# Hybrid encoder block on one core: order of projection units around the recurrence's output transpositions, PSUM banks of the first projection pairs, and the gating loads

## The chip, the cores and the metric

The kernel runs on one core of a Trainium2 chip. The metric is device time of one execution in microseconds, the median over several runs. One execution has been profiled in detail, and every row below comes from it.

## The reference, cut to what matters

One layer of an encoder block for 1024 positions of width 1024, in float32. One large input projection feeds a dilated attention and a bidirectional gated linear attention (GLA); both are merged, and a LayerNorm, a squared-ReLU MLP and a second LayerNorm follow. Around the change this is computed:

```python
proj = x @ w_in
(aq, ak, av, gq, gk, gv, gout, lr_f, lr_b, gate_a, gate_g) = split(proj)
la = log_sigmoid(lr @ w_lr + b_lr) / 16
b = cumsum(la)
q_in, k_in = q * exp(b), k * exp(-b)
o = tri(q_in @ k_in.T) @ v + q_in @ state
o = o * rsqrt(mean(o ** 2) + 1e-6)
y_gla = o * gla_norm_g * silu(gout)
```

GLA has 4 heads with keys of 64 and values of 128 columns, and runs forward and backward over the sequence. The state is carried over chunks.

## The kernel before, in words

**Matmul in three parts.** Every float32 operand is split into a rounded high part and a rest (`halve`, L147; `load_w`, L87: ACT casts, DVE subtracts). `mm3` (L97 to L103) does three matmuls for each 128 rows of the inner dimension: high by high, high by low, low by high. L101 to L103 are therefore the lines of nearly all matmuls.

**Order.** The kernel is written as one program, and a scheduler places each instruction in its engine's queue; it may move an instruction past others of its engine where these are not ready in its own estimate. A block under `issue_after(i)` is queued behind instruction `i` on that engine. In the recurrence, `step` (L506) puts each step's PE work behind the PE work of the step before it, so PE's order there is as written. The engines ACT, DVE, POOL and the DMA queue of SP work their queues in order.

**Recurrence** (L521 to L548). For each of four heads PE does: `turn` twice (transpositions of k, L356), `intra(0)` (scores, L396), `kv` twice (L366), on DVE the chain of `states` (L370), the decays of the next head (`pre1`, L317), `intra(1)`, `out(0)` and `out(1)` (outputs, L407 and L408), `pre2` of the next head, and `outt` twice (transpositions of the normalized outputs, L422). The normalization in `out` is: sums of squares on ACT (L412), a small DVE step (L413), a power on POOL (L414), a product on DVE (L415); then `outt` can start. `outt` writes PSUM tiles of the pool "tr", and ACT copies them out (L424).

**Filling.** Between the steps `fill(n)` (L510) issues units of other projections from a list of 28: 8 of 272 columns, 4 of 512 (queries and keys of heads 2 and 3), 16 of 384 (attention values, `att_v`, L430; sets v0 and v1 of 8). Each has 24 matmuls. `extra` (L493) issues the splits of weights behind the unit with a given count. In every head one unit stands between `intra(0)` and `kv`, one behind `pre1`, one behind `intra(1)`, one between `out` and `outt`; after heads 0 and 2 one more behind `outt`; in head 3 the rest stands ahead of `outt`. The split weights lie in rings of 4 ("whi", "wlo").

**PSUM.** Eight banks: three "mm", two "sc", two "tr", one "av".

**First pairs of the Strassen projections** (`proj`, L571). All other columns of `x @ w_in` are done two blocks at a time by seven products on quarter matrices; sums of x (`xsum`, T1 to T4) and of weights (`side`) are made on DVE. p0 and p1 compute the output gate of GLA. Their products use the three "mm" banks in turn (L569). p0's sides S1, S2 and S3 are issued behind all sums of x (L905).

**Gating** (`silu`, L870). Eight pieces; each loads the gate and the head's outputs, and takes a sigmoid on ACT and two products on DVE, at one step of the pairs behind p1. Its three tiles come from the rings of attention scores. The rest of the kernel is not touched.

Of the kernel before, what the change touches and what calls it, by code (L numbers as in the profile page):

```python
# [7 lines left out]
F32 = mybir.dt.float32  # L8
F32R = mybir.dt.float32r
BF16 = mybir.dt.bfloat16  # L10
I32 = mybir.dt.int32
AF = mybir.ActivationFunctionType
OP = mybir.AluOpType
# [6 lines left out]
KT = D // 128  # L20
# [27 lines left out]
def turns(tiles, n):  # L48

    count = itertools.count()  # L50
    return lambda: tiles[next(count) % n]
# [20 lines left out]
def build(tc, io):  # L72
    nc = tc.nc
    V, G, A, T, SP = nc.vector, nc.gpsimd, nc.scalar, nc.tensor, nc.sync
    P = Pools(tc)
    issued = {}
# [5 lines left out]
    scp = P.open("sc", bufs=2, space=PSUM)  # L82
    trp = P.open("tr", bufs=2, space=PSUM)
# [3 lines left out]
    def load_w(src, shape, raw=None):  # L87
        if raw is None:
            raw = wp.tile(shape, F32, tag="raw", bufs=2, name="raw")
            issued["raw"] = SP.dma_start(raw, src)  # L90
        hi = wp.tile(shape, F32R, tag="whi", bufs=4, name="whi")
        A.copy(hi, raw)
        lo = wp.tile(shape, F32R, tag="wlo", bufs=4, name="wlo")
        V.tensor_tensor(lo, raw, hi.bitcast(F32), op=OP.subtract)  # L94
        return hi, lo
# [9 lines left out]
    def mmtile(w=512):  # L105
        return mmp.tile([128, w], F32, tag="mm", name="mm")

    spill = dr.tile([36, 128, S], F32, name="spill")
    yodr = dr.tile([4, 128, S], F32, name="yodr")
    ygdr = dr.tile([4, 128, S], F32, name="ygdr")  # L110
# [36 lines left out]
    def halve(hi, lo, raw, eng=None):  # L147
        (eng or A.copy)(hi, raw)
        V.tensor_tensor(lo, raw, hi.bitcast(F32), op=OP.subtract)
# [17 lines left out]
    for k in range(KT):  # L167
# [5 lines left out]
        else:  # L173
            if k % 2 == 1:
                n = 2 if k < 7 else 1
# [45 lines left out]
    def piece4(name, dtype=F32, shape=(128, S), parts=128):  # L221
        return kp4.tile([parts, *shape[1:]], dtype, tag="k4", bufs=10, name=name)
# [85 lines left out]
    for i in range(2):  # L308
        sl = slice(i * 512, i * 512 + 512)
# [4 lines left out]
    def gla_head(h):  # L314
# [102 lines left out]

        def outt(half):
            on = st["on", half]
            tp = trp.tile([128, 4, 128], F32, tag="tr", name="tr")  # L420
            for c in range(4):
                issued["pe"] = T.transpose(tp[:, c], on[:, c], ident)  # L422
            o = stg.tile([128, 512], F32, tag="stg", name="yo")
            A.activation(o, tp.rearrange("p c t -> p (c t)"), AF.Copy, scale=cols[:, 32 + h:33 + h])  # L424
            SP.dma_start(yodr[h, :, half * 512:half * 512 + 512], o)
# [2 lines left out]


    def att_v(c):  # L430
        w, raws = [], []

        def fetch_raw(i):
            raws.append(xr_t()[:, 0:768].rearrange("p (k f) -> p k f", k=2))
            with tc.issue_after(issued["raw"].ins):
                SP.dma_start(raws[i], io["wtv"][c, i])

        def split(i):
            w.append(load_w(io["wtv"][c, i], [128, 2, 384], raws[i] if raws else None))

        def unit(t):
            r = c * 8 + t - 2
            if 0 <= r < 12:

                with tc.issue_after(issued["raw"].ins):
                    SP.dma_start(tdr[r], trow[r:r + 1].to_broadcast([128, 512]))
            ps = mmtile(384)
            ts = slice(t * 128, t * 128 + 128)
            mm3(ps, [(xh(k, ts), xl(k, ts), w[k // 2][0][:, k % 2], w[k // 2][1][:, k % 2])
                     for k in range(KT)])  # L450
            o = stg.tile([128, 384], F32, tag="stgv", bufs=2, name="stgv")
            A.copy(o, ps)
            SP.dma_start(vdr[ts, c * 384:c * 384 + 384], o)
        return fetch_raw, split, [lambda t=t: unit(t) for t in range(8)]
# [17 lines left out]
    def xsum(nm, k):  # L472
# [7 lines left out]
        if nm != "T4":  # L480
# [12 lines left out]
    extra = {1: [q_load, k_load], 9: [lambda: split0(0), lambda: split0(1)], 10: [lambda: split0(2)],  # L493
             11: [lambda: split0(3)], 13: [lambda: raw1(0), lambda: raw1(1)],
             14: [lambda: raw1(2), lambda: raw1(3)],
             19: [lambda i=i: split1(i) for i in range(4)]}
    for i, (k, n) in enumerate(((0, 0), (1, 0), (2, 0), (3, 0), (0, 1), (1, 1), (2, 1))):
        extra.setdefault(20 + i // 2, []).append(lambda k=k, n=n: after_raw(xload, k, n))
    count = itertools.count()
# [10 lines left out]
    def fill(n):  # L510
        for _ in range(n):
            step(fills.pop(0))
            for f in extra.pop(next(count), ()):
                f()
# [6 lines left out]
    for h, H in enumerate(heads):  # L521
        more = heads[h + 1:h + 2]
        step(H["turn"], 0)
        step(H["turn"], 1)
        step(H["intra"], 0)
        fill(1)
        step(H["kv"], 0)
        step(H["kv"], 1)
        issued["states"] = H["states"]()
        for N in more:  # L530
            step(N["pre1"])
        fill(1)
        step(H["intra"], 1)
        fill(1)
        step(H["out"], 0)
        step(H["out"], 1)
        for N in more:
            N["pre2"]()
        if not more:
            with tc.issue_after(issued["states"].ins):  # L540
                for k in range(4):
                    xsum("T1", k)
        fill(1 if more else len(fills))
        step(H["outt"], 0)
        step(H["outt"], 1)
        if h in (0, 2):
            fill(1)
    with tc.issue_after(issued["on"].ins):  # L548
        for k in range(3):
            xsum("T3", k)  # L550
    for f in (f for n in sorted(extra) for f in extra[n]):
# [13 lines left out]
          for t, n, d in (("whi", 4, F32R), ("wlo", 4, F32R), ("raw", 2, F32))]  # L565
    p_raw = turns(wt[2] + wt[0][:2], 4)
    p_side = turns([wt[1][0], wt[1][1], wt[0][2], wt[1][2], wt[0][3], wt[1][3],
                    px], 7)
    banks = turns([mmtile() for _ in range(3)], 3)  # L569

    def proj(blocks, r, ahead):  # L571

        st, c, ps = {}, {}, {}

# [111 lines left out]
    NP = len(todo)  # L686
    projs = []
    for i, (bl, r) in enumerate(todo):
        projs.append(proj(bl, r, (lambda i=i: projs[i + 2]["raw"]()) if i + 2 < NP else None))


    p0, p1 = projs[:2]
# [2 lines left out]
    for p, n in ((p0, 0), (p1, 0), (p0, 2), (p1, 2)):  # L695
        prep, do = p["steps"][n]
        prep()
        for f in do:
            f()
    with tc.issue_after(issued["on"].ins):  # L700
        for k in range(4):
            if k == 3:
                xload(k, 1)
                xsum("T3", k)
            xsum("T2", k)
# [163 lines left out]

    def silu(h, hf):  # L870
        sl = slice(hf * 512, hf * 512 + 512)
        g, y, sg = (n().rearrange("p a b -> p (a b)") for n in (e_t, et_t, e_t))
        SP.dma_start(g, spill[4 + h, :, sl])
        SP.dma_start(y, yodr[h, :, sl])
        A.activation(sg, g, AF.Sigmoid)
        with tc.issue_after(issued["add"].ins):
            V.tensor_tensor(y, y, g, op=OP.mult)
            V.tensor_tensor(y, y, sg, op=OP.mult)
        SP.dma_start(ygdr[h, :, sl], y)

    tiles = [att(g, t) for g in (2, 1, 0) for t in range(8)]

# [4 lines left out]
                tiles[n][part]()  # L887


    a, b = p0["steps"][1], p0["steps"][4]  # L890
    steps = [(a[0], b[1]), p0["steps"][3], (b[0], a[1]), *p0["steps"][5:]] + [p1["steps"][n] for n in (1, 3, 4, 5, 6)]
    n0 = len(steps) + 14
    for p in projs[2:]:
        steps += p["steps"]
# [3 lines left out]
        units.setdefault(n0 + 1 + i * (n1 - n0) // 27, []).append(lambda i=i: visit(i))  # L898
    for i in range(8):

        units.setdefault(n0 - 12 + i, []).append(lambda i=i: silu(i // 2, i % 2))
    units[n0].append(tiles[0][0]) if n0 in units else units.setdefault(n0, [tiles[0][0]])
    for i in range(3):
        steps[i][0]()
    fed = []  # L905
    wbt, pa = {}, {}

# [819 lines left out]
```

## Time and profile before

| what | value |
|---|---|
| median of 3 runs | 1412.26 us (1409.19 to 1415.08) |
| the profiled execution | 1410.22 us |
| its span, first to last instruction | 1408.4 us |
| mean granted TensorE clock | 0.994 of full |
| PE busy | 1377.2 us, 98% |
| DVE busy | 1012.7 us, 72% |
| ACT busy | 627.4 us, 45% |

Engines: PE is TensorE's matmuls, PEld its weight loads, DVE VectorE, ACT ScalarE, POOL GpSimd, SP the queue that issues the DMAs. L422 is line 422 of the kernel. In a timeline, the bracket tells how long the engine was idle just ahead of the row, and what ended that.

### The profile page before, as it was taken

Reading aid. Unit: us, or ns where it says so; the run is one execution under the profiler, and the core shown is the slowest. Engines: PE = TensorE matmul, PEld = TensorE weight load, DVE = VectorE, ACT = ScalarE, POOL = GpSimd, SP = SyncE. Lnnn points to the kernel's source line nnn. Section 1 sums busy time; section 2 is a strip of 40 time slices with the busy share of each in tenths; the row PEclk is TensorE's granted clock in tenths of the full one; section 3 lists DMA queues with packets and bytes.
Section 4 is the critical chain, followed back from the end, with each engine's and each line's share of the span. In section 5 each row is a group of like instructions: output and inputs, shape, how many; then the busy total and the mean of one; then the engine's idle time right before and its main releaser. Section 6 shows DMA issues by size and latency. Waiting matters only on the chain.

```text
span 1408.4 us, 18961 instructions
## 1 busy us (share of the span) xinstructions
PE 1377.2 (98%) x6818; PEld 1153.5 (82%) x6818; DVE 1012.7 (72%) x1756; ACT 627.4 (45%) x1194; POOL 24.9 (2%) x41
## 2 busy tenths in 40 slices
PE   8999889999999999999999999999999999999996
PEld 6988888787888888888888888887888888888885
DVE  6375668676655678567766787777867898786988
ACT  5344546235344344354425655454556533333332
POOL 0000000000000000000000000000000000000002
PEclk9999999999999999999999999999999999999999
DMA  7262135484544444375753655656654965545313
GB/s 238 71 205 68 42 105 178 169 254 139 182 141 135 151 164 125 105 239 176 279 212 120 239 182 200 209 195 215 239 195 159 334 241 148 181 120 160 100 40 120
DMA packets 125977, 238.45 MB, mean 169 GB/s; under 512 B 21069, under 2 KB 54093, under 8 KB 125884
## 3 DMA queue, kind: packets, MB, share of 16 engines
q1 hardware_dynamic: 125740, 237.05, 50.4%
q8 instruction: 54, 0.88, 0.3%
q14 instruction: 39, 0.32, 0.1%
q10 hardware_dynamic: 144, 0.20, 0.0%
HBM read 160.57 MB, written 77.68 MB: 169 GB/s over the span
## 4 chain that ended last, share of the span: by engine, by line
PE 88%; DVE 7%; DMA 2%; ACT 2%; issue 1%; POOL 0%; DVEq 0%; SPq 0%; ACTq 0%; POOLq 0%
PE ps L101 17%; PE ps L103 17%; PE ps L102 17%; PE mm L101 10%; PE mm L102 10%; PE mm L103 9%; PE avp L816 3%; PE sc L781 2%; PE tr L802 1%; DVE L L332 0%; DVE L L331 0%; DMA xraw<-in_xT 0%; PE ps L1146 0%; POOL ss L414 0%; DMA fwlo<-in_w 0%
## 5 line engine op out<-in xcount | busy, mean ns | idle before, releaser
L1130 ACT CAST T<-hp 128x1024 fp32r<-128x1024 f32 x36 | 37.8, 1050 | 110.4 <-PE ps L102 70.7
L101 PE MATMUL mm<-whi,x 128*128 128x272 f32 (+1 forms) x256 | 82.0, 320 | 0.4 <-DVE q L269 0.4
L102 PE MATMUL mm<-wlo,x 128*128 128x272 f32 (+1 forms) x256 | 80.4, 314 | 1.3 <-DVE wlo L94 1.3
L103 PE MATMUL mm<-whi,x 128*128 128x272 f32 (+1 forms) x256 | 80.6, 315 | 0.0
L102 PE MATMUL ps<-B,B 128*128 128x512 f32 x160 | 62.4, 390 | 0.0
L103 PE MATMUL ps<-B,B 128*128 128x512 f32 x160 | 62.3, 389 | 0.0
L101 PE MATMUL ps<-B,B 128*128 128x512 f32 x160 | 61.0, 391 | 0.5 <-ACT B L1130 0.5
L625 DVE TENSOR_TENSOR cr<-cu,mm 128x512 f32<-128x512 f32 x48 | 38.0, 791 | 29.1 <-PE mm L103 28.5
L103 PE MATMUL ps<-B,T 128*128 128x512 f32 x144 | 56.2, 390 | 0.0
L101 PE MATMUL ps<-B,T 128*128 128x512 f32 x144 | 56.2, 390 | 0.0
L103 PE MATMUL ps<-T,T 128*128 128x512 f32 x144 | 56.1, 390 | 0.0
L101 PE MATMUL ps<-T,T 128*128 128x512 f32 x144 | 56.0, 389 | 0.0
L102 PE MATMUL ps<-T,T 128*128 128x512 f32 x144 | 56.0, 389 | 0.0
L102 PE MATMUL ps<-B,T 128*128 128x512 f32 x144 | 56.0, 389 | 0.0
L1131 DVE TENSOR_TENSOR T<-hp,T 128x1024 fp32r<-128x1024 f32 x36 | 44.0, 1221 | 15.3 <-ACT T L1130 15.3
L1530 DVE TENSOR_TENSOR acc<-ps,acc 128x512 f32<-128x512 f32 x68 | 45.6, 686 | 13.0 <-PE ps L103 12.2
L791 ACT ACTIVATE e<-e,sm 128x256 f32<-128x256 f32 (+2 forms) x96 | 43.1, 451 | 26.4 <-DVE sm L786 26.2
L1249 ACT ACTIVATE c<-c,cols 128x512 f32<-128x512 f32 x48 | 34.7, 724 | 44.2 <-DVE c L1295 30.0
L101 PE MATMUL mm<-x,pwlo 128*128 128x512 f32 x128 | 51.4, 401 | 0.9 <-DVE cu L625 0.9
L101 PE MATMUL ps<-T,fraw 128*128 128x512 f32 x128 | 50.6, 396 | 1.2 <-DVE c L1289 0.9
L101 PE MATMUL mm<-xT,pwlo 128*128 128x512 f32 x128 | 51.1, 400 | 0.0
L101 PE MATMUL mm<-xT,pwhi 128*128 128x512 f32 x124 | 49.5, 399 | 1.6 <-DVE cu L625 1.3
(440 smaller groups left out, 4105.9 us busy)
## 6 DMA issues: line engine op xcount, KB each, us to landing
hdr<-c SPq DMA_DIRECT2D x112, 256.0 KB, 2.1
hp<-hdr SPq DMA_DIRECT2D x56, 512.0 KB, 3.6
spill<-cr SPq DMA_DIRECT2D x64, 256.0 KB, 2.8
praw<-in_wfm SPq DMA_DIRECT2D x16, 512.0 KB, 4.5
pwhi<-in_wfm SPq DMA_DIRECT2D x16, 512.0 KB, 5.2
gate<-spill SPq DMA_DIRECT2D x32, 256.0 KB, 3.7
wa<-in_w SPq DMA_DIRECT2D x16, 512.0 KB, 4.7
wb<-in_w SPq DMA_DIRECT2D x16, 512.0 KB, 7.2
```

What stands on the lines that cost most here:

```text
L101: T.matmul(ps, lh, rh, start=first and i == 0, stop=False, skip_group_check=more)
L102: T.matmul(ps, lh, rl, start=False, stop=False, skip_group_check=more)
L103: issued["pe"] = T.matmul(ps, ll, rh, start=False, stop=last and i == n - 1, skip_group_check=more)
L625: issued["add"] = V.tensor_tensor(o, a, b, op=OP.add)
L781: T.matmul(sps[i][:, pr, 0:w], q[ps_, pr], k[ps_, pr, 0:w], start=True, stop=True)
L791: issued["exp"] = A.activation(e, e, AF.Exp, bias=sm[:, h:h + 1], scale=-1.0, accum_out=sm[:, 4 + h:5 + h])
L802: T.transpose(tp[0:hi - lo, pr, j], b["e"][i][:, pr, lo:hi], ident)
L816: return T.matmul(av[:, h * 64:h * 64 + 64], b["et"][h % 2][p0:p0 + vv.shape[0], h // 2, j], vv[:, h * 64:h * 64 + 64], start=j == h == 0, ...
L1130: A.copy(o[:, 0], src)
L1131: V.tensor_tensor(o[:, 1], src, o[:, 0].bitcast(F32), op=OP.subtract)
L1249: A.activation(q, src, AF.Relu, bias=cols[:, 2 * j + f:2 * j + f + 1])
L1530: V.tensor_tensor(m, p, m, op=OP.add)
```

## The change

`outt` takes its PSUM tiles from "sc" in place of "tr". Two units stand between `out` and `outt` of heads 0 to 2; the unit behind `outt` of heads 0 and 2 is gone from there, and head 1 has none between `intra(0)` and `kv`. The fourth weight piece of v1 gets two tiles of its own from the pool of 10 pieces (L222), is split behind unit 17 and is used first in each unit of v1. p0 and p1 rotate over seven banks, the other pairs over three. S1, S2 and S3 of p0 are issued ahead of the sums T2 and T4 and the last of T3. The gating's loads are issued two steps ahead of its arithmetic, into the rings of attention keys and values.

```diff
--- before.py
+++ after.py
@@ -417,7 +417,7 @@
 
         def outt(half):
             on = st["on", half]
-            tp = trp.tile([128, 4, 128], F32, tag="tr", name="tr")
+            tp = scp.tile([128, 4, 128], F32, tag="sc", name="sc")
             for c in range(4):
                 issued["pe"] = T.transpose(tp[:, c], on[:, c], ident)
             o = stg.tile([128, 512], F32, tag="stg", name="yo")
@@ -428,7 +428,7 @@
 
 
     def att_v(c):
-        w, raws = [], []
+        w, raws, order = {}, [], (0, 1, 2, 3) if c == 0 else (3, 0, 1, 2)
 
         def fetch_raw(i):
             raws.append(xr_t()[:, 0:768].rearrange("p (k f) -> p k f", k=2))
@@ -436,7 +436,12 @@
                 SP.dma_start(raws[i], io["wtv"][c, i])
 
         def split(i):
-            w.append(load_w(io["wtv"][c, i], [128, 2, 384], raws[i] if raws else None))
+            if c and i == 3:
+
+                w[i] = [piece4(f"wv{p}", F32R, (128, 2, 384)) for p in range(2)]
+                halve(*w[i], raws[i])
+            else:
+                w[i] = load_w(io["wtv"][c, i], [128, 2, 384], raws[i] if raws else None)
 
         def unit(t):
             r = c * 8 + t - 2
@@ -447,7 +452,7 @@
             ps = mmtile(384)
             ts = slice(t * 128, t * 128 + 128)
             mm3(ps, [(xh(k, ts), xl(k, ts), w[k // 2][0][:, k % 2], w[k // 2][1][:, k % 2])
-                     for k in range(KT)])
+                     for i in order for k in (2 * i, 2 * i + 1)])
             o = stg.tile([128, 384], F32, tag="stgv", bufs=2, name="stgv")
             A.copy(o, ps)
             SP.dma_start(vdr[ts, c * 384:c * 384 + 384], o)
@@ -493,7 +498,7 @@
     extra = {1: [q_load, k_load], 9: [lambda: split0(0), lambda: split0(1)], 10: [lambda: split0(2)],
              11: [lambda: split0(3)], 13: [lambda: raw1(0), lambda: raw1(1)],
              14: [lambda: raw1(2), lambda: raw1(3)],
-             19: [lambda i=i: split1(i) for i in range(4)]}
+             17: [lambda: split1(3)], 19: [lambda i=i: split1(i) for i in range(3)]}
     for i, (k, n) in enumerate(((0, 0), (1, 0), (2, 0), (3, 0), (0, 1), (1, 1), (2, 1))):
         extra.setdefault(20 + i // 2, []).append(lambda k=k, n=n: after_raw(xload, k, n))
     count = itertools.count()
@@ -523,7 +528,8 @@
         step(H["turn"], 0)
         step(H["turn"], 1)
         step(H["intra"], 0)
-        fill(1)
+        if h != 1:
+            fill(1)
         step(H["kv"], 0)
         step(H["kv"], 1)
         issued["states"] = H["states"]()
@@ -540,11 +546,9 @@
             with tc.issue_after(issued["states"].ins):
                 for k in range(4):
                     xsum("T1", k)
-        fill(1 if more else len(fills))
+        fill(2 if more else len(fills))
         step(H["outt"], 0)
         step(H["outt"], 1)
-        if h in (0, 2):
-            fill(1)
     with tc.issue_after(issued["on"].ins):
         for k in range(3):
             xsum("T3", k)
@@ -566,9 +570,12 @@
     p_raw = turns(wt[2] + wt[0][:2], 4)
     p_side = turns([wt[1][0], wt[1][1], wt[0][2], wt[1][2], wt[0][3], wt[1][3],
                     px], 7)
-    banks = turns([mmtile() for _ in range(3)], 3)
-
-    def proj(blocks, r, ahead):
+
+    mm_t = [mmtile() for _ in range(3)]
+    more_t = [p.tile([128, 512], F32, tag=t, name=t) for p, t in ((scp, "sc"), (trp, "tr")) for _ in range(2)]
+    banks_of = [turns(mm_t + more_t, 7), turns(mm_t[1:] + mm_t[:1], 3)]
+
+    def proj(blocks, r, ahead, banks):
 
         st, c, ps = {}, {}, {}
 
@@ -686,7 +693,7 @@
     NP = len(todo)
     projs = []
     for i, (bl, r) in enumerate(todo):
-        projs.append(proj(bl, r, (lambda i=i: projs[i + 2]["raw"]()) if i + 2 < NP else None))
+        projs.append(proj(bl, r, (lambda i=i: projs[i + 2]["raw"]()) if i + 2 < NP else None, banks_of[i > 1]))
 
 
     p0, p1 = projs[:2]
@@ -697,6 +704,10 @@
         prep()
         for f in do:
             f()
+    a, b = p0["steps"][1], p0["steps"][4]
+    steps = [(a[0], b[1]), p0["steps"][3], (b[0], a[1]), *p0["steps"][5:]] + [p1["steps"][n] for n in (1, 3, 4, 5, 6)]
+    for i in range(3):
+        steps[i][0]()
     with tc.issue_after(issued["on"].ins):
         for k in range(4):
             if k == 3:
@@ -869,14 +880,21 @@
 
     def silu(h, hf):
         sl = slice(hf * 512, hf * 512 + 512)
-        g, y, sg = (n().rearrange("p a b -> p (a b)") for n in (e_t, et_t, e_t))
-        SP.dma_start(g, spill[4 + h, :, sl])
-        SP.dma_start(y, yodr[h, :, sl])
-        A.activation(sg, g, AF.Sigmoid)
-        with tc.issue_after(issued["add"].ins):
-            V.tensor_tensor(y, y, g, op=OP.mult)
-            V.tensor_tensor(y, y, sg, op=OP.mult)
-        SP.dma_start(ygdr[h, :, sl], y)
+        b = {}
+
+        def load():
+            b["g"], b["y"], b["s"] = (n().rearrange("p a b -> p (a b)") for n in (kk_t, kv_t, e_t))
+            SP.dma_start(b["g"], spill[4 + h, :, sl])
+            SP.dma_start(b["y"], yodr[h, :, sl])
+
+        def do():
+            g, y, sg = b["g"], b["y"], b["s"]
+            A.activation(sg, g, AF.Sigmoid)
+            with tc.issue_after(issued["add"].ins):
+                V.tensor_tensor(y, y, g, op=OP.mult)
+                V.tensor_tensor(y, y, sg, op=OP.mult)
+            SP.dma_start(ygdr[h, :, sl], y)
+        return load, do
 
     tiles = [att(g, t) for g in (2, 1, 0) for t in range(8)]
 
@@ -887,8 +905,6 @@
                 tiles[n][part]()
 
 
-    a, b = p0["steps"][1], p0["steps"][4]
-    steps = [(a[0], b[1]), p0["steps"][3], (b[0], a[1]), *p0["steps"][5:]] + [p1["steps"][n] for n in (1, 3, 4, 5, 6)]
     n0 = len(steps) + 14
     for p in projs[2:]:
         steps += p["steps"]
@@ -898,10 +914,9 @@
         units.setdefault(n0 + 1 + i * (n1 - n0) // 27, []).append(lambda i=i: visit(i))
     for i in range(8):
 
-        units.setdefault(n0 - 12 + i, []).append(lambda i=i: silu(i // 2, i % 2))
+        for n, f in zip((n0 - 14 + i, n0 - 12 + i), silu(i // 2, i % 2)):
+            units.setdefault(n, []).append(f)
     units[n0].append(tiles[0][0]) if n0 in units else units.setdefault(n0, [tiles[0][0]])
-    for i in range(3):
-        steps[i][0]()
     fed = []
     wbt, pa = {}, {}
```

## Rows read from the trace of the kernel before

**Rows 1.** The page: its first line and its row of busy times.
```profile
span 1408.4 us, 18961 instructions
PE 1377.2 (98%) x6818; PEld 1153.5 (82%) x6818; DVE 1012.7 (72%) x1756; ACT 627.4 (45%) x1194; POOL 24.9 (2%) x41
```

**Rows 2.** Waits of PE over the whole span: waiter, releaser, us in total, times, longest.
```profile
PE tr L422 <- DVE on L415: 6.4, 4, 2.3
...
PE mm L101 <- DVE cu L625: 2.2, 2, 1.3
...
PE mm L103 <- DVE pwlo L149: 0.8, 1, 0.8
```

**Rows 3.** Timeline of PE, heads 0 to 3: start, busy, line, tile, count [idle before].
```profile
113.50 0.63 PE L422 MATMUL tr<-ident,on 128*128 128x128 f32 x4 [1.56 <-DVE ss L413]
115.40 0.63 PE L422 MATMUL tr<-ident,on 128*128 128x128 f32 x4 [1.27 <-DVE on L415]
...
121.60 1.04 PE L356 MATMUL tr<-ident,k 128*128 128x128 f32 x8
...
123.66 0.44 PE L101 MATMUL mm<-whi,x 128*128 128x384 f32 x1
...
127.95 1.95 PE L366 MATMUL tr<-gv,kt 128*128 128x128 f32 x16
...
149.31 0.63 PE L422 MATMUL tr<-ident,on 128*128 128x128 f32 x4 [1.58 <-ACT zb L348]
152.27 1.09 PE L422 MATMUL tr<-ident,on 128*128 128x128 f32 x4 [2.33 <-DVE on L415]
153.15 2.10 PE L356 MATMUL tr<-ident,k 128*128 128x128 f32 x8
...
157.19 0.48 PE L101 MATMUL mm<-whi,x 128*128 128x384 f32 x1
...
179.66 0.45 PE L102 MATMUL mm<-wlo,x 128*128 128x384 f32 x1 [1.29 <-DVE wlo L94]
...
184.58 0.63 PE L422 MATMUL tr<-ident,on 128*128 128x128 f32 x4 [1.70 <-DVE on L415]
186.32 0.63 PE L422 MATMUL tr<-ident,on 128*128 128x128 f32 x4 [1.10 <-DVE on L415]
...
224.76 1.03 PE L422 MATMUL tr<-ident,on 128*128 128x128 f32 x8
```

**Rows 4.** Busy time by stretch; the column after POOL is the granted clock.
```profile
116.00:120.00 4.00, 4.00 (x16) 4.00 (x15) 0.82 (x2) 0.69 (x1) 0.00 (x0) 0.57 0.84 245
...
153.00:158.00 5.00, 5.00 (x30) 4.12 (x29) 0.09 (x1) 2.44 (x4) 0.00 (x0) 0.57 0.14 52
...
184.00:188.00 4.00, 2.31 (x15) 2.14 (x16) 3.30 (x4) 2.72 (x5) 0.69 (x1) 1.00 0.67 250
```

**Rows 5.** Timeline of DVE, heads 0 to 2: start, busy, line, tile, count.
```profile
115.17 0.95 DVE L94 TENSOR_TENSOR wlo<-raw,whi 128x768 fp32r<-128x768 f32 x1
...
149.31 1.23 DVE L349 TENSOR_TENSOR q<-q,zb 128x1024 f32<-128x1024 f32 x1
151.43 0.69 DVE L415 TENSOR_TENSOR on<-tr,ss 128x512 f32<-128x512 f32 x1 [0.90 <-POOL ss L414]
...
178.65 2.70 DVE L94 TENSOR_TENSOR wlo<-xraw,whi 128x768 fp32r<-128x768 f32 x3
```

**Rows 6.** Timeline of POOL: the powers of heads 0 and 1.
```profile
113.51 1.02 POOL L414 TENSOR_TENSOR ss<-ss,mhalf 128x4 f32<-128x4 f32 x1 [1.61 <-DVE ss L413]
...
149.39 2.01 POOL L414 TENSOR_TENSOR ss<-ss,mhalf 128x4 f32<-128x4 f32 x1 [1.72 <-DVE ss L413]
```

**Rows 7.** Timeline of ACT: the copy of a head's transposed outputs out of PSUM.
```profile
116.07 0.69 ACT L424 ACTIVATE yo<-tr,cols 128x512 f32<-128x512 f32 x1 [1.16 <-PE tr L422]
```

**Rows 8.** Busy time where the first two pairs begin: PE, PEld, DVE, ACT, POOL, clock.
```profile
222.00:234.00 12.00, 11.18 (x57) 9.50 (x56) 11.49 (x20) 9.90 (x19) 0.00 (x0) 1.00 0.67 235
```

**Rows 9.** DMA issues of the page: stores of projected blocks, KB, us to landing.
```profile
spill<-cr SPq DMA_DIRECT2D x64, 256.0 KB, 2.8
```

## The prediction, written before the result

> **What bounds the kernel now.** First the page [rows 1]: PE is busy for 1377.2 of 1408.4 us, so at most 31.2 us of the span are PE idle, and no change of order can give back more than that and what a lowered clock costs. Next the waits of PE [rows 2]: the largest sum in the recurrence is that of the transpositions on L422, which wait for the normalization's product (L415). The timeline of PE gives these waits one by one [rows 3]. In heads 0 to 2 each of the two transpositions waits: 1.56 and 1.27, 1.58 and 2.33, 1.70 and 1.10 us. A unit of v1 waits 1.29 us for a low weight part. Together 10.83 us. One unit runs between `out` and `outt`; the chain of squares, power and product takes longer than one unit. In head 3, where three units stand there, the eight matmuls of both transpositions run in 1.03 us with no wait [rows 3].
>
> Then the clock [rows 4]. [...] Behind head 2's gaps of 1.70 and 1.10 us it stayed at 1.00, so a gap costs clock sometimes only.
>
> **The recurrence, head by head.** Units of measure [rows 3]: a 384-column unit at the full clock is 127.95 - 123.66 = 4.29 us, of 24 matmuls at 0.179; a pair of transpositions without a wait is 1.03.
>
> Head 0: the unit ahead of the pair ends at 113.50 - 1.56 = 111.94, and head 1 begins at 121.60. These 9.66 us hold the pair and one unit of v0, clean 5.32; the rest is 2.83 idle and some 1.5 of slow clock. Afterwards the unit runs inside the wait. It brings a new wait: its fourth weight piece lies in the slot that the key unit just ahead frees, and its low part is done at 115.17 + 0.95 = 116.12 [rows 5]. The unit wants it as its 20th matmul, at 111.94 + 19 x 0.179 = 115.34. With 0.15 for the handover (a product that ends at 152.12 released PE at 152.27) that is 0.9 us of new wait; both transpositions stand behind it and are ready by then (115.40). Gain 9.66 - 5.32 - 0.9 = 3.4.
>
> Head 1: the pair takes from 149.31 - 1.58 = 147.73 to 153.15, 5.42 against 1.03. Is the second unit enough? From the first `kv` (127.95) to 147.73 PE needs 19.78 us; one unit more and the first transposition make 24.6. The second product ends at 151.43 + 0.69 [rows 5], 24.2 behind `kv`, with the handover 24.3. That just covers it. Moving `kv` ahead of the unit changes none of these distances, since `states` and the next head's decays begin behind `kv` in both. I charge 0.3. Gain 4.1.
>
> Head 2: its transpositions and scores of keys run on the slow clock, 157.19 - 153.15 = 4.04 against 123.66 - 121.60 = 2.06 in head 1: gain 2.0 if the gaps ahead are gone. The wait of 1.29 for the low part: the piece that was fourth is split early and used first, so the late one is wanted six matmuls later, 1.07: gain 1.1. Its early split takes one of the three subtractions (2.70 us together) [rows 5] out of the chain ahead of the normalization: 0.90. The second product then releases PE at 186.32 - 0.90 = 185.4, and two units end at 182.88 + 4.29 - 1.07 = 186.1. Both waits go: gain 2.8.
>
> Sum 3.4 + 4.1 + 2.0 + 1.1 + 2.8 = 13.4.
>
> **The PSUM of `outt`.** The "sc" tiles are used next by `intra(0)`, which must wait for both copies out, while the two `turn` steps take 1.0 us [rows 3]. A copy is 0.69 [rows 7], and a unit's own copy stands ahead of them in ACT's queue. Bounds per head: 0 (covered), and 1.4 (both copies in full). Nearer to covered, since they start with the first transposition's end: I take 0.2 for each of three heads, 0.6. In exchange "tr" no longer waits for them.
>
> **The first pairs.** Behind the recurrence PE's next waits are two on L625, 2.2 us, where a product wants a bank that an addition has not freed, and 0.8 for a split of p1's first side [rows 2]. Seven banks take the first two away unless the next product is itself behind that addition; and the second goes if p1's weights load early, which the slot freed by the fourth piece of v1 allows. Against it: DVE is busy for 11.49 of 12 us here [rows 8], and the change puts six operations for S1 to S3 ahead of T2 and T4; at 0.69 each for this size [rows 5] that is 4.1 us by which those sums can come later. Bounds: a gain of 3.0 and a loss of 4.1. In 222 to 234 PE is busy 11.18 us, so DVE, although full, has kept ahead; I take half of the gain, 1.5.
>
> **The gating.** No line of PE's waits names its tiles, so loads two steps ahead save nothing there; they hide waits of ACT. They move 16 loads forward in SP's queue and use the rings of keys and values, which attention wants only after the last piece. Cost nil while weights are loaded two pairs ahead; the price without that cover is in the last rival.
>
> **Sum.** 13.4 - 0.6 + 1.5 = 14.3. The profiled execution took 1410.22 us (span 1408.4), 2.0 below the median of the runs. 1410.2 - 14.3 = 1395.9, so I forecast 1396.
>
> The power on POOL took 1.02 us alone and 2.01 where it began 0.08 us into DVE's product of q [rows 5, 6]. [...]
>
> **Rivals.** *A, two units don't cover it.* The power and the product of q meet in other places, the copies out of "sc" cost their bound, or DVE takes the fourth piece's subtraction at a bad moment. Speaks for it: head 1's margin of 0.3 us. Against: heads 0 and 2 have 0.7 us and more. Price: 4.1 for the copies, 1.0 for a held power in each of three heads, so a gain of 14.3 - 3.5 - 3.0 = 7.8 or less: 1402 to 1405. Chance 0.13.
>
> *B, DVE takes it back.* PE comes 13 us earlier to a stage in which DVE is full [rows 8]; if that work could not start earlier, PE would wait there for nearly all of it: 1410.2 - 1.5 = about 1409. Against: DVE's sums follow head 3's states, which come earlier by as much, and head 3 itself is unchanged. Chance 0.11.
>
> *C, the banks do nothing.* The scheduler's order, or an addition that the next product needs anyway, leaves the three waits of 3.0 us. Then 1410.2 - 12.8 = 1397.4. Chance 0.07. That the other moves don't happen is excluded by the fixed order of PE's steps.
>
> *D, slower.* A gating load placed two steps ahead stands in SP's queue waiting for the store of the block that it reads; stores take 2.8 us to land [rows 9], and behind it wait the next weights and stores. If all eight pieces passed this on to PE, that is 22.4 us: 1395.9 + 22.4 = 1418. It decides only where SP is held for longer than the lead of the weights, two pairs of projections, and the blocks of p0 and p1 are projected before step 10, where the first load stands. Chance 0.05.
>
> **How the numbers follow.** The forecast's own chance is 0.64. The low end, 1390: the whole 13.4 and 3.0, and 4 us for restarts behind gaps, which I haven't counted. The high end, 1405: 13.4 less 4.1 for the copies and less 4.1 on DVE leaves 5.2. The range holds the forecast, C and most of A, some 0.82. A measurement of this kernel tells about 0.5%, 7 us, from no change: below 1405.2 lie the forecast, A and C, 0.84; B is the same, 0.11; D slower, 0.05.
>
> **What would show it.** L422 without idle time in heads 0 to 2; one wait near 0.9 us inside the unit behind the last key unit; clock 1.00 between 110 and 160; head 3 beginning 12 to 14 us sooner, and the same distance at the first attention scores, plus what the banks give. Wrong would be: a new wait on L396 for ACT above 0.5 us, waits on L101 to L103 for x's sums in the first pairs, or SP held at a gating load.

## The result and the profile after

The changed kernel takes 1400.73 us (median of 5 runs, 1396.73 to 1402.09), the kernel before beside it 1410.18 us (5 runs): a ratio of 0.9922 with an interval of 0.9899 to 0.9945, so faster by 0.8%. The profiled execution took 1400.73 us, its span 9.5 us less than in [rows 1]. The forecast was 1396.0, the range 1390 to 1405: the time lies inside, 4.7 us above the forecast.

The page of the changed kernel: first line and busy times.

```profile
span 1398.9 us, 18965 instructions
PE 1374.9 (98%) x6818; PEld 1152.3 (82%) x6818; DVE 1011.7 (72%) x1756; ACT 626.8 (45%) x1194; POOL 24.8 (2%) x41
```

Waits of PE over the span (in total, times, longest). The waits of L422, 6.4 us for the product in [rows 2] and 9.5 with the other releasers in [rows 3], have become 0.7, and both L625 waits are gone. A wait of 3.8 us for an ACT copy is new.

```profile
PE mm L101 <- ACT cr L657: 3.8, 1, 3.8
...
PE sc L422 <- DVE on L415: 0.7, 1, 0.7
```

Timeline of PE, changed kernel (start, busy, line, tile, count, [idle before]); it answers to [rows 3].

```profile
116.41 0.44 PE L102 MATMUL mm<-wlo,x 128*128 128x384 f32 x1 [0.92 <-DVE wlo L94]
...
117.39 1.03 PE L422 MATMUL sc<-ident,on 128*128 128x128 f32 x8
118.26 1.04 PE L356 MATMUL tr<-ident,k 128*128 128x128 f32 x8
119.22 1.71 PE L396 MATMUL sc<-q,k 64*128 64x128 f32 x16
120.86 2.05 PE L366 MATMUL tr<-gv,kt 128*128 128x128 f32 x16
...
146.03 0.63 PE L422 MATMUL sc<-ident,on 128*128 128x128 f32 x4 [0.66 <-DVE on L415]
146.50 1.04 PE L356 MATMUL tr<-ident,k 128*128 128x128 f32 x8
...
171.53 0.44 PE L102 MATMUL mm<-wlo,x 128*128 128x384 f32 x1 [0.27 <-DVE wlo L94]
...
177.74 1.03 PE L422 MATMUL sc<-ident,on 128*128 128x128 f32 x8
178.61 1.04 PE L356 MATMUL tr<-ident,k 128*128 128x128 f32 x8
...
213.76 0.48 PE L101 MATMUL mm<-x,pwlo 128*128 128x512 f32 x1
...
281.61 0.50 PE L101 MATMUL mm<-xT,pwlo 128*128 128x512 f32 x1 [3.84 <-ACT cr L657]
...
282.29 0.63 PE L103 MATMUL mm<-xT,pwlo 128*128 128x512 f32 x1
...
377.97 0.92 PE L792 MATMUL sc<-ak,aq 64*128 64x192 f32 x8
```

Heads 0 and 2 transpose without a wait, head 1 waits 0.66 us. The wait of 1.29 us for a low part in v1 is down to 0.27 (171.53). Turns of later heads begin 3.3, 6.7 and 12.3 us sooner than before (121.60, 153.15 and 190.95). Then 3.84 us are lost in one place, at 281.61, and the matmuls behind it take up to 0.63 us in place of 0.39.

Busy time by stretch (PE, PEld, DVE, ACT, POOL, granted clock, DMA share, GB/s): where [rows 4] had 0.57 the clock is now 1.00, and it falls in 280 to 286 instead.

```profile
110.00:150.00 40.00, 38.42 (x265) 36.44 (x264) 27.32 (x41) 24.00 (x63) 5.27 (x6) 1.00 0.28 91
150.00:180.00 30.00, 29.73 (x202) 28.75 (x201) 22.81 (x35) 18.80 (x43) 2.38 (x4) 1.00 0.32 105
...
280.00:286.00 6.00, 4.39 (x12) 3.50 (x13) 4.55 (x7) 3.23 (x6) 0.00 (x0) 0.72 1.04 311
```

What leads to the new wait is in the chain of waits of the changed kernel (start, us, what). `av<-yodr` loads a head's outputs, `ak<-spill` the gate, and `ygdr<-av` stores a finished piece.

```profile
264.77 3.53 DMA ygdr<-av
...
268.32 3.82 DMA av<-yodr
...
272.16 0.69 DVE av L894
...
274.96 4.87 DMA ak<-spill
...
281.61 0.50 PE mm L101
```

Down to 274.96 nearly all of it is gating: a store must land before its tile takes the next load, the load before the product, the product before the next load of gates, and that before the sigmoid. ACT's timeline shows what is queued behind the sigmoid: a weight cast and the copy that empties a bank of projections.

```profile
279.94 0.63 ACT L892 ACTIVATE e<-ak 128x512 f32<-128x512 f32 x1 [7.73 <-DMA ak<-spill]
280.47 0.60 ACT L148 CAST pwlo<-praw 128x512 fp32r<-128x512 f32 x1
280.98 0.58 ACT L657 COPY cr<-mm 128x512 f32<-128x512 f32 x1
```

PE had been idle since 277.77 (281.61 - 3.84), so the bank was full by then; its copy began 3.2 us later, behind the sigmoid.

In SP's queue, in 225 to 300, a gating load stood for up to 8.7 us until a product had freed its tile, and three waited for the store of the block that they read. The longest hold ends at 262.96, some 19 us ahead of 281.61.

```profile
SPq L887 <- DVE av L894: 10.5, 4, 8.7
...
SPq L887 <- DMA spill<-cr: 6.2, 3, 2.8
```

**A ledger of three stages.** Every profile has the same three marks on PE: head 0's first turn (first row of L356), p0's first product (first 128x512 row behind the recurrence), and the first 192-wide score of attention. Distances between them are free of where the span begins. Kernels are named by the labels of the experiments below.

| kernel | turn to p0 | p0 to score | score to end |
|---|---|---|---|
| before | 144.93 | 161.97 | 1020.9 |
| changed | 132.91 | 164.21 | 1020.9 |
| changed, again (e15) | 132.95 | 163.50 | 1020.2 |
| e3, recurrence alone | 132.95 | 161.18 | 1021.0 |
| e4, banks alone | 142.61 | 162.64 | 1020.4 |
| e2, gating alone | 144.00 | 165.15 | 1019.6 |
| e5, changed, `outt` in "tr" | 133.55 | 164.23 | 1021.8 |
| e8, changed, sigmoids behind a cast | 132.95 | 164.94 | 1019.9 |
| e12, changed, banks for four pairs | 132.93 | 162.99 | 1019.4 |
| e1, all but gating | 132.94 | 161.35 | 1019.8 |
| e7, e3, sigmoids behind a cast | 132.96 | 162.10 | 1021.2 |
| e9, e7 with av and mm | 131.54 | 161.62 | 1020.2 |
| e14, recurrence, av and mm | 131.47 | 161.38 | 1021.5 |
| e13, e14 + banks for four pairs | 131.52 | 160.32 | 1019.8 |

The first stage gave 12.0 us and the second took 2.2 back; the rest didn't move. In the second stage the gating divides the kernels: the six profiles with its loads ahead (changed twice, e2, e5, e8, e12) take 162.99 to 165.15 us, the eight with the old gating 160.32 to 162.64.

### The profile page after: what moved, and what is told of

Read it like the earlier page. It is cut to its first block, busy times and chain, and to the rows that moved or that the text cites. A ratio compares the mean times of both kernels' runs of the same rounds, so it can differ in the third digit from the quotient of the medians.

```text
span 1398.9 us, 18965 instructions
## 1 busy us (share of the span) xinstructions
PE 1374.9 (98%) x6818; PEld 1152.3 (82%) x6818; DVE 1011.7 (72%) x1756; ACT 626.8 (45%) x1194; POOL 24.8 (2%) x41
## 4 chain that ended last, share of the span: by engine, by line
PE 84%; DVE 7%; DMA 5%; ACT 2%; issue 1%; SPq 1%; POOL 0%; DVEq 0%; ACTq 0%; POOLq 0%
PE ps L101 17%; PE ps L103 17%; PE ps L102 17%; PE mm L101 9%; PE mm L102 8%; PE mm L103 8%; PE avp L827 3%; PE sc L792 2%; PE tr L813 1%; DMA xr<-in_xT 1%; DMA spill<-cr 1%; DMA praw<-in_wfm 1%; DMA ak<-spill 1%; DVE L L332 0%; DMA w<-in_w 0%
## 5 line engine op out<-in xcount | busy, mean ns | idle before, releaser
L102 PE MATMUL mm<-wlo,x 128*128 128x272 f32 (+1 forms) x240 | 74.5, 310 | 1.2 <-DVE wlo L94 1.2
L101 PE MATMUL mm<-whi,x 128*128 128x272 f32 (+1 forms) x240 | 75.1, 313 | 0.2 <-DVE q L269 0.2
L103 PE MATMUL mm<-whi,x 128*128 128x272 f32 (+1 forms) x240 | 74.6, 311 | 0.0
L632 DVE TENSOR_TENSOR cr<-cu,mm 128x512 f32<-128x512 f32 x44 | 35.1, 797 | 28.0 <-PE mm L103 27.8
L101 PE MATMUL ps<-T,fraw 128*128 128x512 f32 x128 | 50.4, 395 | 1.3 <-DVE c L1304 1.1
L101 PE MATMUL mm<-x,pwlo 128*128 128x512 f32 x128 | 51.2, 400 | 0.0
L102 PE MATMUL ps<-T,fraw 128*128 128x512 f32 x128 | 50.1, 392 | 0.0
L103 PE MATMUL mm<-x,pwlo 128*128 128x512 f32 x128 | 50.0, 391 | 0.0
```

The lines of the kernel that those rows point to most:

```text
L101: T.matmul(ps, lh, rh, start=first and i == 0, stop=False, skip_group_check=more)
L102: T.matmul(ps, lh, rl, start=False, stop=False, skip_group_check=more)
L103: issued["pe"] = T.matmul(ps, ll, rh, start=False, stop=last and i == n - 1, skip_group_check=more)
L632: issued["add"] = V.tensor_tensor(o, a, b, op=OP.add)
```

## The experiments

### The parts alone: e3, e4, e2

e3 is the kernel before with the recurrence's part of the diff (order of units, v1's fourth piece, `outt` in "sc"). 

```diff
+            tp = scp.tile([128, 4, 128], F32, tag="sc", name="sc")
...
+        fill(2 if more else len(fills))
```

> The kernel before with only the recurrence changed (two units ahead of the transpositions, their PSUM in sc, the fourth piece of v1 early). If the recurrence's parts do in the changed kernel what its trace shows, head 3 begins 12.3 us sooner, the first pairs 11.8, and the waits for banks (2.2 us) stay: 1410.2 - 11.8 = 1398.4. If the entry of the pairs takes some of it back (waits for sums of x), 1402 to 1406.

Measured: 1398.26 us (4 runs), ratio 0.9921 [0.9900, 0.9942]. So this part alone brings all that the whole change brings. Its pieces were not run singly, but for the bank of `outt` (e5). The wait of 0.8 for p1's first side is gone, and the first pairs still wait for a bank, 1.85 and 0.87 us; its PE timeline at the first:

```profile
235.86 0.51 PE L101 MATMUL mm<-xT,pwhi 128*128 128x512 f32 x1 [1.85 <-DVE cu L629]
```

e4 is the kernel before with the seven banks and S1 to S3 ahead of T2 and T4.

```diff
+    banks_of = [turns(mm_t + more_t, 7), turns(mm_t[1:] + mm_t[:1], 3)]
```

> The kernel before with only the seven banks and the sides S1 to S3 ahead of the sums T2 and T4. If banks are what the two waits on L625 are for, those 2.2 us go and the 0.8 for p1's first side stays (its weights' slot comes from the fourth piece, which is unchanged here): 1408.0. If the order of DVE takes it back, or banks don't matter, 1410.2 or more.

Measured: 1409.50 us (10 runs), ratio 1.0008 [0.9993, 1.0023]: no change. The early waits for a bank are gone, one of 1.05 us for p1's first side stays at 228.14, and PE's timeline has a new one in a pair with three banks, with slow matmuls behind it:

```profile
298.44 0.79 PE L101 MATMUL mm<-x,pwlo 128*128 128x512 f32 x1 [2.36 <-DVE cu L628]
299.03 0.63 PE L102 MATMUL mm<-x,pwlo 128*128 128x512 f32 x1
```

e2 is the kernel before with the gating's part.

```diff
+        for n, f in zip((n0 - 14 + i, n0 - 12 + i), silu(i // 2, i % 2)):
+            units.setdefault(n, []).append(f)
```

> The kernel before with only the gating changed (loads two steps ahead, rings of keys and values). Theory G: a PE wait of 3 to 4 us behind an ACT copy appears in the third pair, and the time is 3 to 6 us above the kernel before, 1413 to 1416. Rival B: no wait of PE over 1 us in the third pair, time as before, 1410.

Measured: 1414.43 us (8 runs), ratio 1.0031 [1.0018, 1.0044]. The gating alone costs some 4 us, as theory G said, though PE's wait is for a sum on DVE and not for a copy. PE's timeline, and ACT's just ahead of it:

```profile
262.98 0.76 PE L101 MATMUL mm<-x,pwlo 128*128 128x512 f32 x1 [2.84 <-DVE cu L625]
```

```profile
260.37 0.63 ACT L881 ACTIVATE e<-ak 128x512 f32<-128x512 f32 x1 [2.96 <-DMA ak<-spill]
260.90 0.60 ACT L148 CAST pwhi<-praw 128x512 fp32r<-128x512 f32 x1
```

A sigmoid waits 2.96 us on ACT for its load, a weight cast behind it starts at 260.90 only, DVE's subtraction waits 2.68 us for the cast, the sum that frees the bank stands behind that subtraction and starts at 262.15, and PE waits 2.84 us for the bank.

### Parts undone: e1, e5

e1 is the changed kernel with the gating as before.

```diff
-        for n, f in zip((n0 - 14 + i, n0 - 12 + i), silu(i // 2, i % 2)):
-            units.setdefault(n, []).append(f)
+        units.setdefault(n0 - 12 + i, []).append(lambda i=i: silu(i // 2, i % 2))
```

> The changed kernel with the gating as before (loads and arithmetic in one step, tiles from the rings of scores). Theory G, a gating load late in its ring holds ACT, and behind it a weight cast and a copy out of PSUM that PE needs: the wait of 3.84 us on L101 near 281 us and the stretch at a granted clock of 0.57 behind it (12 matmuls, some 1.6 us) are gone, so 5.4 us faster than the changed kernel: 1395.3. Rival B, the third pair wants a bank or a split too early because seven banks and the recurrence bring PE there sooner: a wait of 3 to 4 us on L101 stays at that place and the time is that of the changed kernel, 1400.7.

Measured: 1398.12 us (4 runs), ratio 0.9922 [0.9902, 0.9943]. The wait of 3.84 is gone and the second stage is 2.2 to 2.9 us shorter than in the two profiles of the changed kernel; in its place stand waits that the changed kernel has not, 1.01 near 274.7 and 2.49 for a bank near 288.4, so by the medians 2.6 us came of the 5.4 expected. By time alone e1 and the changed kernel can't be told apart (the intervals overlap); the rows tell them apart. PE's timeline in e1:

```profile
288.37 0.50 PE L101 MATMUL mm<-x,pwlo 128*128 128x512 f32 x1 [2.49 <-DVE cu L632]
288.71 0.40 PE L102 MATMUL mm<-x,pwlo 128*128 128x512 f32 x1
```

The waits of ACT in 225 to 300, for e1 and then for the changed kernel, show what loading ahead did for ACT:

```profile
ACT e L886 <- DVE et L888: 9.1, 2, 5.1
ACT e L886 <- DMA e<-spill: 8.6, 4, 3.7
...
ACT L886 <- DMA e<-spill: 2.0, 1, 2.0
```

```profile
ACT e L892 <- DMA ak<-spill: 19.5, 6, 7.7
...
ACT e L892 <- DVE pwhi L149: 0.7, 1, 0.7
```

19.7 against 20.2 us: ACT waits as long for the gating as it did, with a longest wait of 7.7 in place of 5.1. SP's queue is held in e1 too, by the stores of the gating:

```profile
SPq L890 <- DVE et L889: 14.2, 5, 8.9
```

e5 is the changed kernel with `outt` back in "tr".

```diff
-            tp = scp.tile([128, 4, 128], F32, tag="sc", name="sc")
+            tp = trp.tile([128, 4, 128], F32, tag="tr", name="tr")
```

> The changed kernel with the transpositions of outputs back in tr, all else as changed. Theory S, the scores of the next head's first half are 1.71 us long in place of 1.16 because they wait for the second copy out of sc: they fall back to 1.16 here, and in exchange the next head's turn waits for the copies, 0.5 to 1.2 us per head; time 0 to 2 us above the changed kernel. Rival: the scores stay at 1.71, so it is not the PSUM tiles, and the time is unchanged.

Measured: 1401.33 us (2 runs), ratio 0.9942 [0.9922, 0.9962]. Its PE timeline in head 1:

```profile
119.29 1.24 PE L356 MATMUL tr<-ident,k 128*128 128x128 f32 x8 [0.34 <-ACT yo L424]
```

The turns now wait for the copies, 0.34 us here, and the scores take 1.16 us again: both effects that theory S names are there, the first smaller than its 0.5 to 1.2. The first stage is 133.55 us, 0.6 longer than with "sc", in one profile each; the times of the two can't be told apart.

### What holds the pairs: e7, e8, e9

e7 is e3, with each sigmoid issued behind the weight cast that is already on its way.

```diff
-        A.activation(sg, g, AF.Sigmoid)
+        with tc.issue_after(issued["cast"].ins):
+            A.activation(sg, g, AF.Sigmoid)
```

> The kernel before with the recurrence changed, the gating as before but for one thing: each sigmoid is queued on ACT behind the weight cast of the step before. Theory H, PE's waits on L629 in the first pairs (1.85 and 0.87 us with the recurrence alone) come from sigmoids that ACT took early and that hold weight casts and so DVE's queue: the wait of 1.85 goes, the other at least in part: 1396.0. Rival K, these are waits for banks as such: both stay, time as the recurrence alone, 1398.3.

Measured: 1398.04 us (4 runs), ratio 0.9913 [0.9897, 0.9930]: no difference from e3. Both waits stay, now 2.21 and 0.87 us, so the theory that sigmoids on ACT cause them fell. For the first, DVE's timeline has the cause:

```profile
234.00 0.69 DVE L617 TENSOR_TENSOR psum<-praw 128x512 f32<-128x512 f32 x1 [2.85 <-DMA praw<-in_wfm]
...
235.21 0.68 DVE L630 TENSOR_TENSOR cu<-cu,mm 128x512 f32<-128x512 f32 x1
```

The sum that frees the bank (L630) stands behind the next pair's S1, which waited 2.85 us for its weights.

e8 is the changed kernel with the edit of e7.

> The changed kernel with each sigmoid of the gating queued on ACT behind the weight cast of the step before; the loads stay two steps ahead. Theory H: ACT no longer stands at a sigmoid whose load waits for a store, so the wait of 3.84 us and the slow clock behind it (1.6) go: 1395.3. Rival Q, the loads in SP's queue and the rings of keys and values are what holds PE: a wait of over 2 us stays in the third or fourth pair, 1398 to 1401.

Measured: 1399.94 us (4 runs), ratio 0.9935 [0.9920, 0.9949], not distinct from the changed kernel. The wait moved and grew; PE's timeline:

```profile
288.82 0.79 PE L101 MATMUL mm<-x,pwlo 128*128 128x512 f32 x1 [4.34 <-DVE cu L633]
```

Rival Q's wait is there, so the order on ACT isn't the root. What is, isn't shown. On DVE the sum stood behind a subtraction that waited 1.20 us for its weights, which explains a part. A gating load held SP for 8.4 us, but until 261.30, and those weights were issued at 281.44; e1, with the old gating, issues the same weights at 281.11.

e9 is e7 with the transposed outputs in the idle bank "av" and one of "mm".

```diff
+            if half == 0:
+                tp = avp.tile([128, 4, 128], F32, tag="av", name="av")
+            else:
+                tp = mmp.tile([128, 4, 128], F32, tag="mm", name="mm")
```

> As e7, with the first transposition of a head's outputs in the bank av and the second in an mm bank, so that the next scores find both sc tiles free. Theory S: the scores of heads 1 to 3 take 1.16 in place of 1.71, 1.65 us in all: 1394.4 if theory H holds as well, 1396.6 if not. Rival: the mm bank or av is wanted by the next unit or output and PE waits there instead: no gain on e7.

Measured: 1397.49 us (4 runs), ratio 0.9915 [0.9900, 0.9930]. The first stage is 131.54 against 132.96 in e7, so 1.4 us are gained there; in the medians it is 0.55, too little to tell.

### Four on one chip: e12, e13, e14, e15

e12 is the changed kernel with seven banks for four pairs.

```diff
-banks_of[i > 1]))
+banks_of[i > 3]))
```

> The changed kernel with one thing more: the seven banks serve the first four pairs in place of the first two. Theory W (where PE waits behind p1, it is because a product wants the third bank back, which only DVE's sum, queued behind the splits that the gating delays, sets free): the wait of 3.84 us near 281.6 and the slow clock behind it (1.6 us) go, about 1400.7 - 5 = 1395 to 1396, and no wait of PE above 1.5 us stands between 255 and 300. Rival (the product waits for its operand, a weight cast that stands behind the held sigmoid on ACT, whatever the banks): a wait of 2 to 4 us stays near 282, and the time is 1399 to 1402.

Measured: 1399.22 us (6 runs), ratio 0.9927 [0.9913, 0.9941], a time that the rival gave. Neither theory held as written: the wait near 282 went, as theory W said, but one nearly as long came at 289.3, and it is for a sum on DVE, not for the weight cast that the rival named. PE's and DVE's timelines:

```profile
289.31 0.80 PE L101 MATMUL mm<-xT,pwlo 128*128 128x512 f32 x1 [3.34 <-DVE cr L632]
```

```profile
287.58 0.69 DVE L894 TENSOR_TENSOR av<-av,ak 128x512 f32<-128x512 f32 x1 [1.09 <-DMA av<-yodr]
288.19 1.06 DVE L632 TENSOR_TENSOR cr<-cu,mm 128x512 f32<-128x512 f32 x1
```

DVE itself waited for gating loads (1.09 us here, and 1.96 ahead of 283.40), and behind them stood a sum that PE needed. By the code, the products `m2`, `m4` and `m3` accumulate onto a bank that must first be read, so more banks can't spare them that read; that this product was `m4` is read from its operands (a sum of x) and its place, not shown.

e14 is e3 with the edit of e9 (`outt` in "av" and "mm"). e13 is e14 with S1 to S3 ahead and seven banks for four pairs, so the changed kernel with the edits of e1 and e12 and the banks of e9. e15 is the changed kernel once more, with no edit.

> The recurrence's part alone, with the transposed outputs in the banks av and mm in place of sc; three banks for all pairs, the gating as before the change. Against the recurrence's part alone (1398.3) the scores of heads 1 to 3 are 0.55 us shorter each: 1396.6 if PE keeps that (1395.5 to 1398), 1398.3 if the next wait takes it. The waits for a bank near 236 and 250 (1.85 and 0.87 us) stay.

Measured: 1395.86 us (5 runs), ratio 0.9906 [0.9889, 0.9922]. PE's timeline in head 1:

```profile
119.58 1.16 PE L396 MATMUL sc<-q,k 64*128 64x128 f32 x16
```

The scores take 1.16 us again and the turns don't wait. The two waits for a bank stay, 1.66 and 0.87 us.

> The recurrence's part, with the transposed outputs in the banks av and mm in place of sc, the gating as before the change, seven banks for the first four pairs, S1 to S3 ahead. Theory W: the waits of 1.01 and 2.49 us, that the changed kernel with the old gating had near 274 and 288, shrink to under 1 us together and the scores in heads 1 to 3 take 1.16 us, so about 1398.1 - 2.5 - 1.2 = 1394.5 (1393 to 1396). Rival (weights and casts come too late there, whatever the banks): 1397 to 1398.5, with a wait of 1.5 us or more between 255 and 300.

Measured: 1394.36 us (4 runs, 1393.70 to 1396.12), ratio 0.9894 [0.9878, 0.9910]: the best here, and inside theory W's range. Between 214 and 299 no wait of PE is above 0.32 us, although a sigmoid still held ACT for 6.2 us and a gating store SP for 9.9. Against e14 the second stage is 1.1 us shorter; the intervals of the two overlap, so what the banks add isn't settled.

> The changed kernel as it is, on the same chip as the three others: 1400.7 (1396.7 to 1402.1), a ratio to the kernel before of 0.990 to 0.9945, and a wait of 2 to 4 us for ACT between 275 and 290. If that wait is missing here, it is chance and no part of the explanation.

Measured: 1402.00 us (6 runs), ratio 0.9947 [0.9932, 0.9962]; the wait is there again, 3.76 us behind a sigmoid for which ACT had waited 7.50. e5 has it too, 3.96 us, so it is no chance. On this chip e13 and e14, both with the old gating and with the transposed outputs in "av" and "mm", are faster than the whole change, with intervals that don't meet.

## Why the prediction was right, and where it was off

**The recurrence (13.4, less 0.6 for the copies).** Right. By the turns, measured from head 0's first turn, heads 0, 1 and 2 gave 3.6, 3.3 and 5.7 us, and head 3 lost 0.55: 12.0 against 12.8. The new wait inside v0's first unit was 0.92 us, forecast 0.9. The clock stayed at 1.00 in 110 to 180. In e2 and e4, which run the old recurrence, this stage took 144.00 and 142.61 us against 144.93, with a granted clock of 0.96 and 1.00 in 110 to 150, so the gain from one execution, 12.0, is 9.7 to 12.0 over three. The size of this term depended on which execution was read. That the order of the units took the waits away is read from the rows: in e3 it came together with the early weight piece.

**Head 1's margin of 0.3.** Too thin: its second transposition waited 0.66 us. The forecast took over the distance of 24.2 us from `kv` to the second product; it was 25.0 (145.19 + 0.69 - 120.86). DVE's timeline shows why, in the kernel before and then in the changed one:

```profile
148.49 0.68 DVE L415 TENSOR_TENSOR on<-av,ss 128x512 f32<-128x512 f32 x1
149.09 0.16 DVE L413 TENSOR_SCALAR ss<-ss 128x4 f32<-128x4 f32 x1
```

```profile
142.11 0.95 DVE L149 TENSOR_TENSOR wv<-xraw,wv 128x768 fp32r<-128x768 f32 x1
142.97 0.16 DVE L413 TENSOR_SCALAR ss<-ss 128x4 f32<-128x4 f32 x1
143.07 1.23 DVE L349 TENSOR_TENSOR q<-q,zb 128x1024 f32<-128x1024 f32 x1
```

The early subtraction of v1's fourth piece, 0.95 us, stands in head 1's chain ahead of L413. The forecast took it out of head 2's chain (0.90) and put it at nothing in head 1's; rival A names the danger. The timeline of POOL, changed kernel, has the power beside the product of q:

```profile
143.28 1.88 POOL L414 TENSOR_TENSOR ss<-ss,mhalf 128x4 f32<-128x4 f32 x1 [2.59 <-DVE ss L413]
```

It began 0.21 us into that product (143.28 - 143.07); the other three powers of heads 0 and 1 took 1.01 to 1.02. But this power took 2.01 before [rows 6], and the 24.2 held that already: it is no part of the 0.66.

**The copies out of "sc" (0.2 per head).** Under-sized. The scores of heads 1 to 3 take 1.71 us in place of 1.16, so 0.55 each, 1.65 in all, inside the bounds of 0 and 1.4 per head. The second half of the scores begins 0.55 us behind the first (119.78 against 119.22 in head 1), where in the kernel before the two began together (122.57 and 122.56). That it waits for the second copy isn't shown: in head 2 that copy had ended at 147.39, and the second half began at 148.02. e14, with the transposed outputs out of "sc", gives 1.5 of it back against e3.

**The first pairs (+1.5, half of 3.0).** The banks took the two waits on L625 away; the third, 0.8 for p1's first side, went with the recurrence's part (gone in e3, 1.05 in e4), where the forecast named the fourth piece's slot. And yet the banks brought nothing: e4 is 1.0008 of before, and e1's second stage is 161.35 us against 161.18 in e3. The step that failed is that a bank wait removed is PE time gained. DVE's sum comes late because it is queued behind other work: near 235 in e7 behind an S1 that waited for weights, and at 288.4 in e1 behind subtractions and a product of the gating, with DVE at work from 282.5 on without a gap above 0.2 us. When the ring is three again, or a product accumulates onto a bank still to be read, PE waits for that sum (2.49 us in e1, 3.34 in e12). DVE's timeline in e1:

```profile
286.43 0.68 DVE L889 TENSOR_TENSOR et<-et,e 128x512 f32<-128x512 f32 x1
...
287.63 0.68 DVE L632 TENSOR_TENSOR cu<-cu,mm 128x512 f32<-128x512 f32 x1
```

**The gating (cost nil while weights are loaded two pairs ahead).** This is the step that failed most. The second stage is 3.2 us longer in e2 than before, and 2.2 to 2.9 us longer in the changed kernel than in e1. The cover named was the lead of the weights on SP. In the changed kernel the price came by another path: the sigmoid stands in ACT's queue ahead of casts and of the copies that free banks, and its load waited for a tile of a ring of three. In e8 and e12 PE's wait is for a sum on DVE.

Why the early loads cost more than the old ones stays open. One estimate fits both: a piece comes every product, 2.73 us (12 matmuls at 0.2275), so a tile may be in use for 3 x 2.73 = 8.2 us, and the tile of a head's outputs needs a load of 3.82, two products of 0.69 and a store of 3.53, together 8.7, without the time its products wait in DVE's queue. But the old gating's ring is three deep too. The eight pieces should follow within 7 x 2.73 = 19.1 us; from the first to the last they take 29.2 in the changed kernel (L894, 262.25 to 291.43) and 31.7 in e1 (L888, 259.98 to 291.71). So both fall behind, and the ring alone doesn't tell them apart. A ring of four wasn't tried.

**The sum.** 14.3 forecast, 9.5 measured: 0.8 of the 4.8 us is the recurrence, 3.7 the second stage (+1.5 forecast, -2.2 measured), and 0.3 lies outside these two stages. No run shows a figure for the 4 us for restarts behind gaps in the range's low end; behind the wait of 2.49 us in e1 the first matmul took 0.50 us and the next 0.40. The time fell inside the range because the largest term was right and the two terms that failed were small.

**The rivals.** Of A one part happened, the fourth piece's subtraction at a bad moment, for 0.66 us; its price of 6.5 us did not. B's mechanism didn't, DVE takes none of the recurrence's gain in e3. C held in its effect (no net gain from the banks), not by its cause, since the waits named did go. D named the gating load in SP's queue and was right that it waits there: three times for the store of its block, 6.2 us in all. But what PE lost was one wait of 3.84 us and slow clock behind it, on ACT's path, not eight times 2.8; the longest hold of SP, 8.7 us, was for a tile, and e1 and e13 have such holds (8.9 and 9.9) with the old gating.

## What to carry to other kernels

Before counting a wait as hidden by a load that is issued ahead, ask whether its tile is free that early: multiply the time between uses by the ring's depth and compare with load, use and store together (here 8.2 against 8.7, an estimate from the times above, and ACT waited 20.2 us against 19.7 with the old gating). When an operation is moved out of one chain, look for the chain that it lands in: 0.95 us taken from head 2 made head 1 wait 0.66. In the changed kernel a sigmoid kept ACT idle for 7.73 us until its load had landed, a cast and a bank's copy came behind it, and PE waited 3.84: look for the bank-freeing copies and sums behind an operation that waits for a DMA. When a wait for a buffer is removed, ask what made its release late: in e4 the waits on L625 went, and one of 2.36 us stood in a pair with three banks.

## What the runs showed of the hardware

The same idle time does not always cost clock. Behind waits of 3.84 (changed), 3.34 (e12), 2.84 (e2) and 2.36 us (e4) matmuls of 512 columns took 0.63 us (the granted clock was 0.72 over 280 to 286 in the changed kernel, and 0.57 over 281.6 to 284.5); behind 2.49 us in e1 they took 0.40, with the clock at 1.00. So the length of the gap alone doesn't decide; what else does isn't settled here. And the same code ran 116 to 120 at a clock of 0.57 in the profile of before, at 0.60 in e2 and at 1.00 in e4. A gain that consists of slow clock should be read from more than one execution.

In the gating, loads of 256 KB took 3.82 and 4.87 us and a store 3.53 in the changed kernel, where the DMA share was 0.75 over 264 to 280, against 2.8 for the median store in [rows 9].
